# A planner gives the VectorE/GpSimd lock to more operations, and re-ranks by its own plan: a hybrid decoder trunk on one core

## The chip, the core and the metric

The kernel runs on one core of a Trainium2 chip. A core has TensorE (PE: matrix products), VectorE (DVE), ScalarE (ACT), GpSimd (POOL) and SyncE (SP, which issues the transfers here); each works through its own queue of instructions in order, and they meet only at semaphores. SBUF is the on-chip memory that all of them read, PSUM holds the results of TensorE. The metric is the time of one execution on the device in microseconds (us), the median of several runs.

## The reference

Two layers of a decoder trunk on a 1024 x 1024 float32 input. In each layer one input projection feeds four token mixers, whose outputs are normalised, joined, projected and added; then comes a SwiGLU feed-forward block.

```python
for l in range(DEPTH):                      # 2 layers
    h = rmsnorm(x, attn_norm[l])
    proj = h @ w_in[l]                      # 1024 -> 1952 columns, split among the mixers
    y_a = mla_attention(...)                # causal, 4 heads, rotary key
    y_b = short_gated_conv(...)             # width 3
    y_c = multiscale_pool(...)              # trailing means over 2, 4, 8, 16
    y_d = swa_sink_attention(...)           # window 128, sinks, softmax per 128-row block
    mixed = group_rmsnorm(y_a, y_b, y_c, y_d) * mix_norm[l]
    x = x + mixed @ w_o[l]
    h2 = rmsnorm(x, ffn_norm[l])
    gate, up = jnp.split(h2 @ w_gate_up[l], 2, axis=-1)      # 1024 -> 2 x 2816
    x = x + (silu(gate) * up) @ w_down[l]
return rmsnorm(x, final_norm)
```

## The kernel before

Activations are kept transposed, channels on the 128 partitions and 512 tokens in a tile. A product in float32 is made of three fast ones: every operand is split into a rounded high part (a cast on ScalarE, line 301) and the remainder (a subtraction on VectorE, line 304), and TensorE adds high x high, high x low and low x high (the matmuls of line 281). The feed-forward block uses a Strassen-like scheme (the names B11, N1, T3 and so on), whose sums and differences of weights and activations are made on VectorE and, in part, on GpSimd.

The places that matter below, in each of the two layers:

- **Sliding-window attention** (`swa_unit`, 16 units a layer). TensorE makes the scores of a unit (line 594), VectorE adds the bias and finds the row's maximum (line 604), ScalarE takes the exponential (line 617), VectorE adds the sink's part (lines 627, 629, on tiles of 128 x 2), takes the reciprocal (630) and scales the two 128 x 256 halves of the probabilities `tp` by it (line 632, TENSOR_SCALAR); then TensorE transposes them (line 643) and multiplies them with the values (line 655). The matmuls of line 281 that stand between these belong to later projections and fill TensorE's time meanwhile.
- **Sums of two gate/up weight blocks** (`premake`, lines 768 to 776), made early for the feed-forward block: two loads, four GpSimd additions of 128 x 512 (lines 770 to 773), two stores. It is done twice a layer, so eight GpSimd operations stand one behind another.
- **Entry to the feed-forward block.** VectorE makes sums of the normalised activations (lines 1153, 1166, 1172, 1174), splits them and the first weights (line 304, the weights as 128 x 1024), and combines residual tiles (lines 380, 1283); a few additions run on GpSimd (line 1479).

The order of each engine's queue is not written by hand. `scheduled_kernel` records the program once, and `Order` builds a graph of its instructions with two durations for each: `seen` (until its result can be used) and `taken` (until its engine is free). `_forward` is a list scheduler: at each step the engine that is free first takes, of its ready instructions, the one with the smallest rank. It also carries a few shared things, among them `lock`: an operation whose kind is TWO (VectorE) or POOL (a GpSimd TENSOR_TENSOR) begins only when the one before it has released the lock. `find` repeats this with ranks from a backward pass. From its plan PSUM banks and the 47 SBUF slots are given to the tiles (`banks`, `spans`), which adds dependencies of its own, and the program is recorded again; this is done for five rounds, and the round with the shortest plan is kept. Then `_search` perturbs the ranks 1500 times and keeps what `_trials` finds better, the mean of four plans with drawn transfer delays. The order that is left is imposed on the queues.

A GpSimd TENSOR_TENSOR had the kind POOL. On VectorE only a two-tensor operation (TENSOR_TENSOR or SCALAR_TENSOR_TENSOR), both of its inputs with more than two elements a partition, had the kind TWO, when none of these lies in PSUM.

## Time and profile before

| | before |
|---|---|
| median of 3 runs | 2063.58 us (2062.7 to 2064.33) |
| the profiled execution: its time, its span | 2065.29 us, 2063.5 us |
| busy share: TensorE, VectorE, ScalarE, GpSimd | 99%, 76%, 48%, 28% |
| transfers: mean rate over the span | 147 GB/s |

The span runs from the first to the last instruction of the profiled execution; the execution's own time has 1.8 us around it. Each row of a timeline has the start in us, the time in us, engine, line, operation, output and inputs, shape, the count of merged instructions, and, in brackets, how long the engine had stood idle before it and who ended that. Matmuls are pipelined, so that their ends are modelled: the distance from one start to the next says what one costs. Names of tiles stand without their numbers (`u` is a slot of SBUF, `ps_` a PSUM tile). A row of the windows view has, for each engine, the busy time in that stretch and the count of instructions.

### The profile page before, as it was taken

Reading aid. Unit: us, or ns where it says so; the run is one execution under the profiler, and the core shown is the slowest. Engines: PE = TensorE matmul, PEld = TensorE weight load, DVE = VectorE, ACT = ScalarE, POOL = GpSimd, SP = SyncE. Lnnn points to the kernel's source line nnn. Section 1 sums busy time; section 2 is a strip of 40 time slices with the busy share of each in tenths; the row PEclk is TensorE's granted clock in tenths of the full one; section 3 lists DMA queues with packets and bytes.
Section 4 is the critical chain, followed back from the end, with each engine's and each line's share of the span. In section 5 each row is a group of like instructions: output and inputs, shape, how many; then the busy total and the mean of one; then the engine's idle time right before and its main releaser. Section 6 shows DMA issues by size and latency. Waiting matters only on the chain.

```text
span 2063.5 us, 26530 instructions
## 1 busy us (share of the span) xinstructions
PE 2036.2 (99%) x9422; PEld 1679.0 (81%) x9422; DVE 1564.7 (76%) x2443; ACT 992.0 (48%) x1737; POOL 568.5 (28%) x420
## 2 busy tenths in 40 slices
PE   9999999999999999999999999999999999999998
PEld 7787888778888888888887878888788888888887
DVE  8879978998777678655657899789876767785546
ACT  7447647753333334444434476577433333354332
POOL 0100000037687683000001000000578768710000
PEclk9999999999999999999999999999999999999999
DMA  5301222434555556766403002243355555486542
GB/s 207 128 21 36 76 81 83 160 105 169 183 181 172 182 184 240 260 218 222 160 31 125 31 25 89 67 128 118 109 191 175 184 182 178 165 310 239 186 161 100
DMA packets 142117, 302.36 MB, mean 147 GB/s; under 512 B 13856, under 2 KB 60960, under 8 KB 141984
## 3 DMA queue, kind: packets, MB, share of 16 engines
q1 hardware_dynamic: 141984, 300.66, 43.1%
q8 instruction: 74, 1.21, 0.2%
q14 instruction: 59, 0.48, 0.1%
HBM read 212.00 MB, written 87.56 MB: 145 GB/s over the span
## 4 chain that ended last, share of the span: by engine, by line
PE 87%; DVE 6%; ACT 3%; issue 2%; DMA 1%; POOL 0%; SPq 0%; DVEq 0%; ACTq 0%; POOLq 0%
PE ps_mm L281 34%; PE ps_s L281 26%; PE ps_t L281 10%; PE ps_pv L281 8%; PE ps_pv L1065 2%; PE ps_t L1053 1%; DVE u L304 1%; PE ps_s L999 1%; DVE u L307 1%; PE ps_s L1001 1%; PE ps_s L1000 1%; DMA u<-in_w_gu 1%; PE ps_s L871 1%; PE ps_pv L655 1%; ACT u L306 1%
## 5 line engine op out<-in xcount | busy, mean ns | idle before, releaser
L281 PE MATMUL ps_mm<-u,u 128*128 128x512 f32 (+1 forms) x3378 | 839.3, 391 | 4.2 <-DVE u L304 1.7
L281 PEld LDWEIGHTS ps_mm<-u,u 128*128 128x128 f32 x3378 | 618.5, 189 | 130.9 <-issue 5.4
L281 PE MATMUL ps_s<-u,u 128*128 128x512 f32 x2670 | 639.7, 390 | 3.1 <-ACT u L301 1.0
L304 DVE TENSOR_TENSOR u<-u,u 128x1024 fp32r<-128x1024 f32 (+2 forms) x400 | 477.3, 1210 | 167.7 <-ACT u L301 101.8
L281 PEld LDWEIGHTS ps_s<-u,u 128*128 128x128 f32 x2670 | 500.4, 188 | 112.1 <-ACT u L301 2.6
L301 ACT CAST u<-u 128x1024 fp32r<-128x1024 f32 (+2 forms) x400 | 346.8, 882 | 479.0 <-PE ps_s L281 121.5
L281 PE MATMUL ps_t<-u,u 128*128 128x512 f32 (+1 forms) x1124 | 255.8, 377 | 0.5 <-ACT u L306 0.5
L281 PEld LDWEIGHTS ps_t<-u,u 128*128 128x128 f32 x1124 | 202.7, 188 | 40.3 <-ACT u L306 1.3
L1479 POOL TENSOR_TENSOR tp<-tp,u 128x512 f32<-128x512 f32 x80 | 132.3, 1654 | 338.5 <-ACT tp L1477 338.5
L281 PE MATMUL ps_pv<-u,u 128*128 128x512 f32 x744 | 179.2, 389 | 0.1
L281 PEld LDWEIGHTS ps_pv<-u,u 128*128 128x128 f32 x744 | 139.5, 188 | 29.8 <-ACT tn L1342 0.6
L1062 POOL MEMSET u<- 128x128 f32 x32 | 5.7, 206 | 497.9 <-PE ps_mm L281 324.9
L770 POOL TENSOR_TENSOR u<-u,u 128x512 f32<-128x512 f32 x4 | 5.3, 1316 | 373.1 <-PE ps_s L594 288.1
L1477 ACT ACTIVATE tp<-tp 128x512 f32<-128x512 f32 x80 | 50.5, 632 | 109.1 <-DVE tp L380 108.9
L301 ACT CAST u<-ps_t 128x512 fp32r<-128x512 f32 (+3 forms) x132 | 64.4, 502 | 64.3 <-PE ps_t L643 30.1
L304 DVE TENSOR_TENSOR u<-ps_t,u 128x512 fp32r<-128x512 f32 (+3 forms) x132 | 74.5, 580 | 13.6 <-ACT u L301 12.7
L1264 POOL TENSOR_TENSOR u<-u 128x512 f32<-128x512 f32 x38 | 77.8, 2048 | 20.8 <-DVE u L304 20.8
L306 ACT ACTIVATE u<-u,par 128x512 fp32r<-128x512 f32 x100 | 69.8, 715 | 25.5 <-DVE u L380 11.8
L1557 POOL TENSOR_TENSOR u<-u 128x352 f32<-128x352 f32 x64 | 80.6, 1260 | 2.4 <-DMA u<-in_w_dn 1.3
L307 DVE SCALAR_TENSOR_TENSOR u<-u,par,u 128x512 fp32r<-128x512 f32 x100 | 72.9, 746 | 5.0 <-ACT u L306 4.8
L1557 POOL TENSOR_TENSOR u<-u,u 128x352 f32<-128x352 f32 x64 | 74.6, 1165 | 3.6
L345 ACT ACTIVATE tn<-u 128x512 f32<-128x512 f32 (+1 forms) x91 | 52.3, 595 | 43.3 <-DVE u L1750 41.0
(206 smaller groups left out, 2377.2 us busy)
## 6 DMA issues: line engine op xcount, KB each, us to landing
u<-in_w_gu SPq DMA_DIRECT2D x92, 512.0 KB, 3.6
ad<-u SPq DMA_DIRECT2D x154, 256.0 KB, 2.1
u<-ad SPq DMA_DIRECT2D x70, 512.0 KB, 5.8
u<-in_w_dn SPq DMA_DIRECT2D x64, 352.0 KB, 3.2
qd<-u SPq DMA_DIRECT2D x64, 352.0 KB, 3.0
u<-qd SPq DMA_DIRECT2D x32, 512.0 KB, 5.2
u<-in_w_in SPq DMA_DIRECT2D x28, 512.0 KB, 3.8
u<-in_w_dn SPq DMA_DIRECT2D x24, 512.0 KB, 6.5
```

The lines of the kernel that those rows point to most:

```text
L281: pe.matmul(o, w, r, start=start and k == 0 and i == 0, stop=stop and k == n - 1 and i == 2, skip_group_check=again,)
L301: a = act.copy(hi, f)
L304: dve.tensor_tensor(out=lo, in0=f, in1=rd(hi), op=ALU.subtract)
L306: a = act.activation(hi, f, AF.Copy, scale=gain)
L307: dve.scalar_tensor_tensor(out=lo, in0=f, scalar=gain, in1=rd(hi), op0=ALU.mult, op1=ALU.subtract)
L345: act.activation(q, f, AF.Square)
L655: pe.matmul(py[:, (i % 2) * 256 : (i % 2 + 1) * 256], v, R.ap(tt)[:, kb * 256 : (kb + 1) * 256], start=n == 0, stop=n == 2 * nkb - 1,)
L1065: pe.matmul(py[:, c0:], v_of(j, h), R.ap(s)[:, c0:], start=j == 0 and n == 0, stop=j == nj - 1 and n == 1,)
L1264: pool.tensor_tensor(out=q4, in0=q4, in1=F.ap(self.raw[1] + 1), op=ALU.add)
L1477: last_silu = act.activation(g, g, AF.Silu)
L1479: pool.tensor_tensor(out=g, in0=g, in1=r, op=ALU.mult)
L1557: pool.tensor_tensor(out=o, in0=a, in1=b, op=ALU.add)
```

## The change

Four things, all in the planner; the instructions of the program are the same in kind and number.

- The kind TWO is given to every VectorE TENSOR_TENSOR, SCALAR_TENSOR_TENSOR, TENSOR_SCALAR and copy whose inputs all lie in SBUF, whatever their number and size. New in it are the one-input operations (line 632 among them) and those on 128 x 2 tiles (lines 627, 629). The time for which such an operation holds the lock is at least 0.05.
- A transpose on TensorE is put down with 0.1135 instead of 0.109.
- Each of the five rounds is now judged by a short search (a tenth of the trials) and not by `find` alone, and the last search starts from the ranks of the round that won.
- A trial is given up as soon as its sum can't come below the best.

```diff
@@ _forward
-            lock = get + seen[k] - (0.16 if kind[k] == TWO else 0.19)
+            lock = get + max(0.05, seen[k] - (0.16 if kind[k] == TWO else 0.19))
@@ _trials
-def _trials(arrays, graph, lates, order):
+def _trials(arrays, graph, lates, order, limit):
...
         total += end.max()
+        if total + (lates.shape[0] - 1 - s) * (limit - 2.0) > lates.shape[0] * limit:
+            return 1e18
@@ _search
-    best = _trials(arrays, graph, lates, order)
+    best = _trials(arrays, graph, lates, order, 1e9)
...
-        got = _trials(arrays, graph, lates, trial)
+        got = _trials(arrays, graph, lates, trial, best)
@@ Order
+    @staticmethod
+    def tensors(i):
+        return [a for a in i.ins if hasattr(a, "memref")]
...
-        two = op == "TensorTensor" or op == "TensorScalarPtr" and i.is_scalar_tensor_tensor
-        if e == "DVE" and two and len(aps) == 2:
-            return 0 if any(a.memref.startswith("ps_") for a in aps) else TWO
+        if e == "DVE" and op in ("TensorTensor", "TensorScalarPtr", "TensorScalar", "TensorCopy"):
+            return 0 if any(str(a.memref).startswith("ps_") for a in cls.tensors(i)) else TWO
...
             if i.is_transpose:
-                return 0.28, 0.109
+                return 0.28, 0.1135
...
-    def search(self, trials, seed=1):
-        rank = self.find()[1]
+    def search(self, trials, seed=1, rank=None):
+        if rank is None:
+            rank = self.find()[1]
@@ scheduled_kernel
-    for _ in range(rounds):
+    for r in range(rounds):
         _, _, begin, end = plan.find()
         given = plan.banks(begin, end), plan.spans(made, begin, end)
         nc, traced, made = trace(*given)
         plan = Order(traced, nc.dependency_edges)
-        found = plan.find()[0]
-        if best is None or found < best[0]:
-            best = found, given, plan
-    order = best[2].search(trials)[1]
-    return trace(*best[1], order)[0]
+        found = plan.search(trials // 10, r)
+        if best is None or found[0] < best[0]:
+            best = found[0], given, plan, found[4], found[1]
+    _, given, plan, rank, rows = best
+    found = plan.search(trials, rounds, rank)
+    return trace(*given, found[1])[0]
```

What it does to the queues is seen in the order of the built programs. The queues are alike at the start (TensorE's first 100 rows or so) and differ from then on; three places are shown.

**TensorE, layer 0, the last two units of sliding-window attention.** `ps_t<-cst,tp` is a transpose of line 643, which needs the `tp` that line 632 has scaled; `ps_mm` with `u_874`, `u_875` is the projection that stands between; three matmuls belong to each of its pieces of weight (`u_206`, `u_218` and so on, starting at `u_156` behind the last scores). Before:

```order
L281 MATMUL ps_mm<-u_218,u_874 128x512 x2
L281 MATMUL ps_mm<-u_218,u_875 128x512
L643 MATMUL ps_t<-cst,tp 128x128
L281 MATMUL ps_mm<-u_230,u_874 128x512
L643 MATMUL ps_t<-cst,tp 128x128 x3
L281 MATMUL ps_mm<-u_230,u_874 128x512
L281 MATMUL ps_mm<-u_230,u_875 128x512
L643 MATMUL ps_t<-cst,tp 128x128
L281 MATMUL ps_mm<-u_242,u_874 128x512
L643 MATMUL ps_t<-cst,tp 128x128 x2
L655 MATMUL ps_pv<-u_908,u_457 128x256
L643 MATMUL ps_t<-cst,tp 128x128
```

Now:

```order
L281 MATMUL ps_mm<-u_304,u_874 128x512 x2
L643 MATMUL ps_t<-cst,tp 128x128
L281 MATMUL ps_mm<-u_304,u_875 128x512
L281 MATMUL ps_mm<-u_316,u_874 128x512 x2
L281 MATMUL ps_mm<-u_316,u_875 128x512
L281 MATMUL ps_mm<-u_328,u_874 128x512
L643 MATMUL ps_t<-cst,tp 128x128 x3
L281 MATMUL ps_mm<-u_328,u_874 128x512
L281 MATMUL ps_mm<-u_328,u_875 128x512
L281 MATMUL ps_mm<-u_340,u_874 128x512 x2
L281 MATMUL ps_mm<-u_340,u_875 128x512
L655 MATMUL ps_pv<-u_908,u_457 128x256
```

From the last scores to the first transpose stand 25 matmuls of 512 columns instead of 17; then 5 instead of 1 to the other three transposes of that unit; the transposes of the last unit, which followed after 2, now follow after 11 (and 4 matmuls of line 655). The first of the GpSimd additions waits for a matmul that stands 21 places ahead of the end of the last scores (5 of 512 columns and 16 of 256), where it waited for one of these scores themselves.

**TensorE, layer 1, the same place** (`u_9594`, `u_9595` is the projection between). Before:

```order
L281 MATMUL ps_mm<-u_8559,u_9594 128x512 x2
L281 MATMUL ps_mm<-u_8559,u_9595 128x512
L643 MATMUL ps_t<-cst,tp 128x128 x4
L281 MATMUL ps_mm<-u_8867,u_9594 128x512 x2
L281 MATMUL ps_mm<-u_8867,u_9595 128x512
L643 MATMUL ps_t<-cst,tp 128x128 x4
L281 MATMUL ps_mm<-u_8628,u_9594 128x512 x2
```

Now:

```order
L655 MATMUL ps_pv<-u_9530,u_9178 128x256 x4
L281 MATMUL ps_mm<-u_8810,u_9594 128x512
L643 MATMUL ps_t<-cst,tp 128x128
L281 MATMUL ps_mm<-u_8810,u_9594 128x512
L281 MATMUL ps_mm<-u_8810,u_9595 128x512
L281 MATMUL ps_mm<-u_8559,u_9594 128x512 x2
L281 MATMUL ps_mm<-u_8313,u_9724 128x512 x2
L643 MATMUL ps_t<-cst,tp 128x128 x3
L281 MATMUL ps_mm<-u_8559,u_9595 128x512
L281 MATMUL ps_mm<-u_8867,u_9594 128x512 x2
L281 MATMUL ps_mm<-u_8867,u_9595 128x512
L281 MATMUL ps_mm<-u_8628,u_9594 128x512 x2
```

The last unit's transposes followed 3 matmuls behind those of the unit before; now 13 matmuls of 512 columns and 4 of 256 stand between. The two rows with `u_8313,u_9724` begin another product, in a PSUM bank that VectorE's line 480 must have read; in VectorE's queue that operation stands right behind the pair of line 632. Of the GpSimd additions the first waits for a matmul that stands 18 places ahead of the end of the first scores (6 of 512 columns, 8 of 256, 4 transposes).

**VectorE, layer 0, entry to the feed-forward block.** `u_4404` (128 x 1024) is the remainder of the first weights. Before:

```order
L380 TENSOR_TENSOR tp<-ps_t,u_3957 128x512
L1166 SCALAR_TENSOR_TENSOR tp<-u_3186,par,te 128x512
L304 TENSOR_TENSOR u_4340<-tp,u_4340 128x512
L1283 TENSOR_TENSOR u_3957<-ps_t,tn 128x512
L1153 SCALAR_TENSOR_TENSOR tp<-tp,te 128x512
L304 TENSOR_TENSOR u_4404<-u_4401,u_4403 128x1024
```

Now:

```order
L380 TENSOR_TENSOR tp<-ps_t,u_3957 128x512
L1166 SCALAR_TENSOR_TENSOR tp<-u_3186,par,te 128x512
L304 TENSOR_TENSOR u_4340<-tp,u_4340 128x512
L304 TENSOR_TENSOR u_4404<-u_4401,u_4403 128x1024
L1153 SCALAR_TENSOR_TENSOR tp<-tp,te 128x512
L304 TENSOR_TENSOR u_4360<-tp,u_4360 128x512
```

The remainder of the weights has come two places forward, ahead of lines 1283 and 1153. In layer 1 the same operations keep their places, but line 1283 has come ahead of all of them.

## The prediction

> **What bounds the kernel now.** I read the page's first part and its chain first, then the busy time by stretches of the span, then who TensorE waits for, then the timelines of the places where it waits.

> ```profile
> span 2063.5 us, 26530 instructions
> PE 2036.2 (99%) x9422; PEld 1679.0 (81%) x9422; DVE 1564.7 (76%) x2443; ACT 992.0 (48%) x1737; POOL 568.5 (28%) x420
> PE 87%; DVE 6%; ACT 3%; issue 2%; DMA 1%; POOL 0%; SPq 0%; DVEq 0%; ACTq 0%; POOLq 0%
> ```

> TensorE is busy for 2036.2 of 2063.5 us and carries 87% of the chain. The instructions do not change, so the busy time stays; all that another order can win lies in the 27.3 us in which TensorE is idle. Where they are, by stretches (PE first, then weight load, VectorE, ScalarE, GpSimd):

> ```profile
> 0.00:50.00 50.00, 47.84 (x212) 38.25 (x213) 43.97 (x72) 39.40 (x66) 0.20 (x4) 1.00 0.59 213
> 50.00:100.00 50.00, 45.68 (x231) 37.78 (x231) 41.81 (x106) 20.53 (x61) 10.20 (x8) 0.93 0.37 132
> 400.00:500.00 100.00, 97.86 (x421) 79.26 (x420) 90.80 (x108) 48.90 (x75) 43.87 (x29) 0.98 0.35 117
> 500.00:600.00 100.00, 100.00 (x443) 82.84 (x442) 72.34 (x70) 35.04 (x48) 73.82 (x52) 1.00 0.57 185
> 1100.00:1200.00 100.00, 96.69 (x473) 78.92 (x473) 80.81 (x190) 49.89 (x122) 10.18 (x8) 0.98 0.17 61
> 1400.00:1500.00 100.00, 96.94 (x419) 77.43 (x418) 93.17 (x125) 58.67 (x93) 32.54 (x19) 1.00 0.34 118
> 2000.00:2063.50 63.50, 54.10 (x362) 49.63 (x360) 37.15 (x69) 18.99 (x37) 0.00 (x0) 0.94 0.24 82
> ```

> The feed-forward stretch (500 to 600) has no gap: 443 matmuls in 100 us, 0.226 us for one of 512 columns. GpSimd and its lock cost nothing there, however VectorE is slowed. The head (2.16 us idle) and the tail (9.40) are the fill and drain; the queues are alike in the first, and the last chain is the same. That leaves 15.7 us, of which 4.32 lie at 50 to 100, 3.31 at 1100 to 1200, 2.14 and 3.06 at the two entries to the feed-forward block. Who TensorE waits for (total, times, longest):

> ```profile
> PE ps_t L643 <- DVE tp L632: 7.4, 7, 1.7
> PE ps_mm L281 <- DVE u L304: 1.7, 1, 1.7
> ```

> The largest by far is the transposes' wait for line 632. Its place in layer 0: GpSimd's first and last addition, VectorE, and TensorE with its idle time in brackets.

> ```profile
> 85.39 1.30 POOL L770 TENSOR_TENSOR u<-u,u 128x512 f32<-128x512 f32 x1 [84.95 <-DVE u L672]
> 94.64 1.27 POOL L773 TENSOR_TENSOR u<-u 128x512 f32<-128x512 f32 x1
> 84.23 0.69 DVE L380 TENSOR_TENSOR u<-u,te 128x512 f32<-128x512 f32 x1
> 87.08 0.88 DVE L627 TENSOR_TENSOR sm<-sm,par 128x2 f32<-128x2 f32 x1
> 89.57 2.52 DVE L632 TENSOR_SCALAR tp<-tp,sm 128x256 f32<-128x256 f32 x2
> 92.01 1.23 DVE L629 TENSOR_TENSOR sm<-sm,sm 128x2 f32<-128x2 f32 x1
> 93.48 2.58 DVE L632 TENSOR_SCALAR tp<-tp,sm 128x256 f32<-128x256 f32 x2
> 84.37 1.12 PE L594 MATMUL ps_s<-u,u 128*128 128x256 f32 x8
> 85.33 4.04 PE L281 MATMUL ps_mm<-u,u 128*128 128x512 f32 x17
> 90.95 0.30 PE L643 MATMUL ps_t<-cst,tp 128*128 128x128 f32 x1 [1.58 <-DVE tp L632]
> 92.14 0.55 PE L643 MATMUL ps_t<-cst,tp 128*128 128x128 f32 x3 [0.66 <-DVE tp L632]
> 92.45 0.71 PE L281 MATMUL ps_mm<-u,u 128*128 128x512 f32 x2
> 94.86 0.45 PE L643 MATMUL ps_t<-cst,tp 128*128 128x128 f32 x1 [1.70 <-DVE tp L632]
> 96.11 0.69 PE L643 MATMUL ps_t<-cst,tp 128*128 128x128 f32 x2 [0.38 <-DVE tp L632]
> L632 DVE TENSOR_SCALAR tp<-tp,sm x64: 277/347/1429, 53.6 to 1192.1; 128x256 f32<-128x256 f32 x56, 128x128 f32<-128x128 f32 x8
> ```

> A scaling of line 632 takes 347 ns (the median in the last row), but 2.52 for two while GpSimd adds: each waits for the GpSimd operation that is running. So does a 128 x 2 operation of line 629, at 1.23. These are the operations to which the planner gave no lock: it put 17 matmuls (17 x 0.226 = 3.85 us) where 5.6 were needed. In layer 1 the same (GpSimd's first addition, TensorE's three waits, and a VectorE operation used below):

> ```profile
> 1109.96 1.30 POOL L770 TENSOR_TENSOR u<-u,u 128x512 f32<-128x512 f32 x1 [288.12 <-PE ps_s L594]
> 1115.43 0.55 PE L643 MATMUL ps_t<-cst,tp 128*128 128x128 f32 x3 [0.81 <-DVE tp L632]
> 1118.04 0.30 PE L643 MATMUL ps_t<-cst,tp 128*128 128x128 f32 x1 [1.36 <-DVE tp L632]
> 1119.28 0.55 PE L643 MATMUL ps_t<-cst,tp 128*128 128x128 f32 x3 [0.95 <-DVE tp L632]
> 1115.30 0.68 DVE L480 SCALAR_TENSOR_TENSOR te<-ps_mm,u 128x512 f32<-128x512 f32 x1
> ```

> **The change part by part.** No instruction is added or taken away. The floor of 0.05, the transposes' 0.1135, the early end of trials and the seeds cost nothing on the chip, since they act through the order alone.

> *Layer 0, the softmax beside GpSimd.* Waits removed at most: 1.58 + 0.66 + 1.70 + 0.38 = 4.32 us. What stays? I take the end of the scores, 85.33, as the mark. A matmul of 256 columns costs 0.12 ((85.33 - 84.37) / 8), a transpose 0.10 ((92.45 - 92.14) / 3). GpSimd now starts 5 x 0.226 + 16 x 0.12 = 3.05 us earlier against the mark, less the 0.69 for which line 380, ready in that time, takes the lock: 2.4 earlier, so that its last addition ends at 95.91 - 2.4 = 93.5. The two scalings of the first unit ended with GpSimd's fourth and fifth addition (four from 85.39, about 1.32 apart: 90.7; then 92.09). The softmax can't be ready earlier than before (line 627 at 87.08), so it loses two places in GpSimd's row of eight: scalings end with the sixth and seventh addition at 90.9 and 92.2, plus 0.35 each. TensorE comes to the first transpose at 85.33 + 25 x 0.226 = 90.98 and to the other three 0.10 + 5 x 0.226 = 1.23 later, so it waits 0.3 and 0.1. If VectorE misses one place more, 1.3 is added: 1.7 at most. The last unit's transposes come 11 x 0.226 + 4 x 0.12 = 3.0 us later, after GpSimd is done, and wait for nothing. I take 1.0, between the ends: **-3.3** (-4.3 to -2.6; if the shift of GpSimd fails because the second pair of weight blocks lands late, -2).

> *Layer 1.* Waits removed at most: 0.81 + 1.36 + 0.95 = 3.12. GpSimd starts 6 x 0.226 + 8 x 0.12 + 4 x 0.10 = 2.7 us ahead of the first scores' end. The last unit's transposes gain 13 x 0.226 + 4 x 0.12 = 3.4 us, which covers 1.36 + 0.95 whole. The first unit's have 17 + 3 matmuls and 12 of 256 columns (20 x 0.226 = 4.5 + 0.9) against 20 and 4 before, so their wait goes from 0.81 to about nothing. But two matmuls ahead of the last three transposes need a bank that line 480 reads, and that stands behind the two scalings: where these end late, its 0.68 and about 0.4 of a slot at GpSimd come to TensorE, up to 1.1. I take 0.8: **-2.3** (-3.1 to -1).

> *Entry to the feed-forward block.* VectorE is the bound there:

> ```profile
> 400.00:420.00 20.00, 20.00 (x89) 16.19 (x88) 20.00 (x30) 13.91 (x23) 1.30 (x1) 1.00 0.14 46
> 432.49 0.68 DVE L1283 TENSOR_TENSOR u<-ps_t,tn 128x512 f32<-128x512 f32 x1
> 433.09 1.16 DVE L1153 SCALAR_TENSOR_TENSOR tp<-tp,te 128x512 f32<-128x512 f32 x1
> 434.17 1.21 DVE L304 TENSOR_TENSOR u<-u,u 128x1024 fp32r<-128x1024 f32 x1
> 1452.14 3.96 POOL L1479 TENSOR_TENSOR tp<-tp,u 128x512 f32<-128x512 f32 x1 [11.76 <-ACT tp L1477]
> 1456.13 0.69 DVE L380 TENSOR_TENSOR u<-ps_t,tp 128x512 f32<-128x512 f32 x1 [1.19 <-POOL tp L1479]
> ```

> It is busy for 20.00 of 20 us, so TensorE gets its operand as VectorE's queue comes to it. In layer 0 the remainder of the weights comes forward past lines 1283 and 1153, which took 434.17 - 432.49 = 1.68 us. What may take some of it back is the next thing late, line 380 behind a GpSimd addition of line 1479: it stood 1.19 for that in layer 1. So -1.7 to -0.5, and I take **-1.0**. In layer 1 line 1283 has come ahead of the same remainder, which is 433.09 - 432.49 = 0.60 later: **+0.6**.

> [...]

> *All the rest.* 15.7 - 7.4 - 2.1 - 3.1 = 3.1 us of idle time lie scattered; another order makes others of the same kind. I take 0, with 2.5 either way.

> Sum: -3.3 - 2.3 - 1.0 + 0.6 = -6.0. The profiled execution was 2065.29 us (span 2063.5 and 1.8 around it), 1.7 above the median of the runs, 2063.58. So 2059.3 for such an execution, and **2057.6** for the median.

> **The rivals.**

> *The search finds more.* It re-ranks 750 times more and picks the slot plan by a searched time; if it also halves the rest (the 5.2 at the two entries and 3.1 elsewhere), 4 more go: 2053.5. For it: a lock known is a lock that can be planned around. Against: layer 1's entry stands almost as it stood. 15%.

> *The stalls move.* The same 10.2 us of GpSimd work holds off the same VectorE operations; if the second weight pair lands late, or line 480 and the scores behind it take over the wait, about 2 us are won: 2061.6. Against: 25, 5 and 13 matmuls are real cover. 20%.

> *The change does not do what it says*: the lock for one-input operations is a fiction, or binds nowhere. The rows at 89.57 and 92.01 show it binding, and the queues did move there, so this has 2%; the time would be that of a random re-order, 2063.

> *Slower: GpSimd starves behind VectorE's trains.* The planner hands the lock to GpSimd after one VectorE operation; the row at 1452.14 shows 3.96 - 1.30 = 2.66 us lost behind a train of them, with line 380 waiting after it and TensorE behind that. If the new order sends all four additions of line 1479 at the two entries (two in each layer) into such trains, 4 x 2.66 = 10.6 us come back, against the 6.0: 2068.2. It decides from the third on (3 x 2.66 = 8 against 6). Against it: line 1479 has moved by a place or two only. 6%.

> **How the numbers follow.** Likeliest, my sum: 57%, with 2055 to 2060.5 by its terms' ends. Less than 0.2% (4.1 us) can't be told from no change here, so faster means under 2059.5 and slower over 2067.7. Faster: most of the 57% (47) and the 15% of the search: 0.62. Slower: 0.05. The rest, 0.33, is the upper part of the sum's range and the stalls that move. The range reaches to both neighbours, 2052.5 to 2063.

> **What would show it.** In the new profile the wait of line 643 for line 632 should fall from 7.4 to under 3 us; TensorE's busy time at 50 to 100 should rise by about 3 us, and at 1100 to 1200 by 2; GpSimd's first addition should start some 2.5 us ahead of the last scores. At the entries, idle time of about 1 us in layer 0 and 3.7 in layer 1. I am wrong if the wait of line 643 stays over 5, if a new row of TensorE's waits stands over 2 us, or if the 500 to 1000 stretch is no longer full.

## The result, and the profile after

| | before | after |
|---|---|---|
| median (lowest to highest) | 2063.32 us (2062.7 to 2064.33, 4 runs) | 2049.36 us (2049.12 to 2049.48, 4 runs) |
| profiled execution: time, span | 2065.29, 2063.5 us | 2049.12, 2047.3 us |

The ratio is 0.9932 (95% interval 0.9915 to 0.9949). Beside the experiments below both were timed again: 2048.80 against 2066.26 us, ratio 0.9915 (0.9902 to 0.9929). The two medians of before lie 3 us apart, within the 7.6 us over which its runs spread (last section). The direction was as predicted, the size was not: 14.0 us by the medians where 6.0 were forecast, and a time below the range. The span fell by 16.2 us.

The first part of the page of after:

```profile
span 2047.3 us, 26523 instructions
PE 2030.1 (99%) x9422; PEld 1675.2 (82%) x9422; DVE 1552.7 (76%) x2443; ACT 992.3 (48%) x1737; POOL 574.1 (28%) x420
```

TensorE's idle time fell from 27.3 to 17.2 us, that is by 10.1, and its busy time from 2036.2 to 2030.1, by 6.1, with the same 9422 matmuls. The second number is the surprise. After, by the same stretches as in the prediction (span, TensorE's busy time first; the third column from the right is the granted clock):

```profile
50.00:100.00 50.00, 50.00 (x265) 42.22 (x264) 41.08 (x109) 22.64 (x64) 10.62 (x8) 1.00 0.39 132
400.00:500.00 100.00, 98.46 (x429) 79.74 (x428) 84.78 (x100) 48.08 (x72) 56.55 (x36) 1.00 0.42 138
500.00:600.00 100.00, 100.00 (x443) 82.81 (x442) 71.96 (x71) 34.86 (x47) 72.06 (x51) 1.00 0.53 174
1100.00:1200.00 100.00, 99.56 (x479) 80.16 (x478) 85.13 (x191) 56.39 (x127) 5.13 (x5) 1.00 0.14 49
1400.00:1500.00 100.00, 97.14 (x425) 78.75 (x424) 89.39 (x113) 52.58 (x81) 45.15 (x28) 1.00 0.35 120
2000.00:2047.30 47.30, 37.99 (x289) 36.17 (x287) 24.29 (x51) 10.33 (x22) 0.00 (x0) 0.95 0.25 90
```

At 50 to 100 no idle time is left, at 1100 to 1200 0.44 us, and the clock, which read 0.93, 0.98 and 0.98 in three of these rows before, is 1.00 everywhere but in the tail. Who TensorE waits for now, longest first:

```profile
PE ps_mm L281 <- DVE u L304: 1.9, 2, 1.7
PE ps_s L281 <- DVE u L304: 1.6, 2, 0.9
PE ps_pv L497 <- DVE ones L155: 1.1, 1, 1.1
```

The row of line 643 waiting for line 632 (7.4 us before) is gone; what leads now is the wait at the entry to the feed-forward block and the drain. The place in layer 0, in the timeline of after:

```profile
83.49 1.30 POOL L770 TENSOR_TENSOR u<-u,u 128x512 f32<-128x512 f32 x1 [83.05 <-PE ps_mm L281]
93.12 1.30 POOL L773 TENSOR_TENSOR u<-u 128x512 f32<-128x512 f32 x1
89.64 0.74 DVE L629 TENSOR_TENSOR sm<-sm,sm 128x2 f32<-128x2 f32 x1
91.55 1.64 DVE L632 TENSOR_SCALAR tp<-tp,sm 128x256 f32<-128x256 f32 x2
85.86 0.64 PE L594 MATMUL ps_s<-u,u 128*128 128x256 f32 x4
86.34 5.86 PE L281 MATMUL ps_mm<-u,u 128*128 128x512 f32 x25
92.04 0.30 PE L643 MATMUL ps_t<-cst,tp 128*128 128x128 f32 x1
93.33 0.49 PE L643 MATMUL ps_t<-cst,tp 128*128 128x128 f32 x3
```

The scalings still stand behind GpSimd (1.64 us for two), but 25 matmuls run meanwhile, and the transposes come when their operands are there: no brackets, no idle time.

### The profile page after: what moved, and what is told of

Its sections match the earlier page's. It is cut to its first block, busy times and chain, and to the rows that moved or that the text cites. A ratio compares the mean times of both kernels' runs of the same rounds, so it can differ in the third digit from the quotient of the medians.

```text
span 2047.3 us, 26523 instructions
## 1 busy us (share of the span) xinstructions
PE 2030.1 (99%) x9422; PEld 1675.2 (82%) x9422; DVE 1552.7 (76%) x2443; ACT 992.3 (48%) x1737; POOL 574.1 (28%) x420
## 3 DMA queue, kind: packets, MB, share of 16 engines
q8 instruction: 74, 1.21, 0.2%
## 4 chain that ended last, share of the span: by engine, by line
PE 86%; DVE 7%; ACT 2%; issue 2%; DMA 1%; POOL 0%; SPq 0%; DVEq 0%; ACTq 0%; POOLq 0%
PE ps_mm L281 33%; PE ps_s L281 27%; PE ps_t L281 10%; PE ps_pv L281 8%; PE ps_pv L1065 2%; PE ps_t L1053 1%; DVE u L307 1%; DVE u L304 1%; PE ps_s L999 1%; DVE u L353 1%; PE ps_s L1000 1%; PE ps_s L1001 1%; PE ps_s L871 1%; PE ps_pv L655 1%; PE ps_s L594 1%
## 5 line engine op out<-in xcount | busy, mean ns | idle before, releaser
L281 PE MATMUL ps_mm<-u,u 128*128 128x512 f32 (+1 forms) x3378 | 835.4, 390 | 2.6 <-DVE u L304 1.9
L281 PEld LDWEIGHTS ps_mm<-u,u 128*128 128x128 f32 x3378 | 614.9, 188 | 129.8 <-issue 4.6
L281 PE MATMUL ps_s<-u,u 128*128 128x512 f32 x2670 | 636.8, 390 | 2.4 <-DVE u L304 1.6
L304 DVE TENSOR_TENSOR u<-u,u 128x1024 fp32r<-128x1024 f32 (+2 forms) x400 | 470.5, 1192 | 175.5 <-ACT u L301 107.7
L281 PEld LDWEIGHTS ps_s<-u,u 128*128 128x128 f32 x2670 | 500.4, 188 | 110.0 <-DVE u L304 2.4
L281 PE MATMUL ps_t<-u,u 128*128 128x512 f32 (+1 forms) x1124 | 255.9, 377 | 0.1
L281 PEld LDWEIGHTS ps_t<-u,u 128*128 128x128 f32 x1124 | 202.5, 188 | 40.5 <-DVE u L307 0.9
L1479 POOL TENSOR_TENSOR tp<-tp,u 128x512 f32<-128x512 f32 x80 | 139.5, 1744 | 337.4 <-ACT tp L1477 337.4
L281 PE MATMUL ps_pv<-u,u 128*128 128x512 f32 x744 | 178.3, 389 | 0.1
L281 PEld LDWEIGHTS ps_pv<-u,u 128*128 128x128 f32 x744 | 139.3, 188 | 29.9 <-ACT tn L1342 1.0
L770 POOL TENSOR_TENSOR u<-u,u 128x512 f32<-128x512 f32 x4 | 5.2, 1292 | 365.9 <-PE ps_mm L281 365.9
L1477 ACT ACTIVATE tp<-tp 128x512 f32<-128x512 f32 x80 | 50.5, 632 | 97.1 <-DVE tp L380 97.0
L304 DVE TENSOR_TENSOR u<-ps_t,u 128x512 fp32r<-128x512 f32 (+3 forms) x132 | 75.0, 581 | 15.1 <-ACT u L301 13.9
L380 DVE TENSOR_TENSOR tp<-tp,u 128x512 f32<-128x512 f32 x76 | 71.8, 945 | 2.0
```

The lines of the kernel that those rows point to most:

```text
L281: pe.matmul(o, w, r, start=start and k == 0 and i == 0, stop=stop and k == n - 1 and i == 2, skip_group_check=again,)
L304: dve.tensor_tensor(out=lo, in0=f, in1=rd(hi), op=ALU.subtract)
L380: dve.tensor_tensor(out=o, in0=a, in1=b, op=ALU.mult)
L1477: last_silu = act.activation(g, g, AF.Silu)
L1479: pool.tensor_tensor(out=g, in0=g, in1=r, op=ALU.mult)
```

## Where 6 us of busy time went

TensorE's clock had been halved three times inside the kernel before. The profile keeps the granted clock as intervals: before it was 0.5 at 93.14 to 99.97, 434.47 to 437.89 and 1120.55 to 1123.97 us, after at no time between 5 us and the drain. All of these are one or two times 3.413 us long, and they start on one grid of 3.413 us. Before, cut on that grid (clock in the third column from the right, TensorE's busy time first behind the length):

```profile
89.73:93.14 3.41, 1.52 (x7) 0.83 (x7) 3.41 (x3) 0.78 (x4) 3.41 (x3) 1.00 0.47 193
93.14:96.56 3.42, 1.34 (x6) 0.85 (x5) 3.35 (x5) 0.23 (x1) 2.61 (x3) 0.50 0.62 216
96.56:99.97 3.41, 3.41 (x13) 2.97 (x12) 1.79 (x4) 1.62 (x3) 0.00 (x0) 0.50 0.61 245
99.97:103.38 3.41, 3.41 (x18) 2.85 (x17) 1.80 (x4) 1.07 (x4) 0.00 (x0) 1.00 0.00 0
431.06:434.47 3.41, 1.78 (x6) 0.59 (x4) 3.41 (x6) 1.87 (x4) 1.39 (x1) 1.00 0.00 0
434.47:437.89 3.42, 2.94 (x7) 2.37 (x8) 3.42 (x6) 0.42 (x1) 0.00 (x0) 0.50 0.43 137
1117.14:1120.55 3.41, 1.57 (x8) 1.28 (x9) 2.75 (x4) 0.59 (x1) 3.15 (x3) 1.00 0.48 181
1120.55:1123.97 3.42, 3.42 (x11) 2.84 (x11) 2.00 (x3) 1.23 (x2) 0.00 (x0) 0.50 0.83 302
```

Each of the three windows at full clock ahead of a half-clock one here had TensorE idle for 1.63 to 1.89 us by its busy time (over 2.1 by the distances between starts, last section). At half clock matmuls of 512 columns begin 0.427 us apart, where they begin 0.227 apart at full clock, and count as busy: 11 matmuls fill the 3.42 us of the last row. The busy time of the four half-clock windows is 1.34 + 3.41 + 2.94 + 3.42 = 11.1 us; half of that, 5.6 by the granted clock of 0.50, is the clock's, and TensorE's busy time fell by 6.1. (The difference is small beside the modelled ends: the profiles of all the kernels below that keep at most one half-clock window and have no matmuls or holds added show busy times from 2028.6 to 2030.5.) So a stall was paid twice: once as idle time, and again in the 3.4 us behind it. That this is so, and that the lock is behind it, had to be tested.

## The experiments

The theories: **A**, the planner's knowledge of the lock puts matmuls ahead of the waiting transposes, and this takes away both the idle time and the half clock behind it. **B**, the half clock costs nothing of its own; **C**, it has nothing to do with the idle time; **D**, the gain is the search's; **E**, any other order moves by some us; **F**, line 632 is late for other reasons than GpSimd. The kernel before, timed beside these runs, had medians of 2066.26 to 2066.67 us; the ratios are against those.

### TensorE kept busy in the stall, in the plan of before

```diff
+FILL = {  # layer, group, unit: (matmuls, unit and transpose they stand ahead of)
+    (0, 0, 6): ((6, 6, 0),),
+    (0, 0, 7): ((2, 6, 1), (7, 7, 0)),
+    (1, 0, 7): ((3, 6, 1), (5, 7, 0)),
+}
...
+                    m = pe.matmul(pt, ones_r, R.ap(vs[g][1]), start=True, stop=True)
```

> The plan of before, unchanged, with 23 matmuls of 512 columns (5.2 us of TensorE's time, results overwritten) put ahead of the transposes that wait for line 632. VectorE, GpSimd and all waits for line 632 stay, so no work is ready earlier; only TensorE isn't idle there. Theory A (the idle time itself was only part of the loss, and the clock that is halved behind it the rest): the granted clock is 1.00 at 84 to 105 and 1105 to 1124, TensorE's busy time without the fillers falls by some 3.5 us, and the time is 2058 to 2061. Rival B (the clock's dip costs nothing of its own, since TensorE would have waited there anyway): 2063 to 2065. Rival C (the dips have nothing to do with the idle time): the clock dips at the same places.

Measured: 2060.52 us (2059.6 to 2060.89), ratio 0.9968 (0.9956 to 0.9981). The kernel does 23 matmuls more and is faster. The first part of its page:

```profile
span 2059.0 us, 26573 instructions
PE 2038.2 (99%) x9445; PEld 1682.9 (82%) x9445; DVE 1568.1 (76%) x2443; ACT 991.9 (48%) x1737; POOL 568.7 (28%) x420
```

The two softmax stretches (columns as above):

```profile
50.00:100.00 50.00, 48.82 (x255) 40.44 (x255) 42.51 (x106) 20.73 (x62) 10.27 (x8) 1.00 0.36 132
1100.00:1200.00 100.00, 98.51 (x484) 80.34 (x483) 82.33 (x190) 51.35 (x123) 10.21 (x8) 1.00 0.17 61
```

The transposes' wait for the scalings (lines 654 and 639 here):

```profile
PE ps_t L654 <- DVE tp L639: 2.1, 3, 1.0
```

The clock is 1.00 in both stretches; the half-clock interval at the entry (433.90 to 437.31), where no matmul was put, stays. Without the fillers' 5.2 us TensorE is busy for 2033.0, 3.2 less than before. B and C fall: idle time was the cause of the half clock, and the half clock cost time.

### GpSimd's additions made short, in the plan of before

```diff
+            c = slice(0, 8 if narrow else HT)
+            kept = w1 if narrow else q
...
-            pool.tensor_tensor(out=F.ap(q + 1), in0=a21, in1=a22, op=ALU.add)
+            pool.tensor_tensor(out=q1[:, c], in0=a21[:, c], in1=a22[:, c], op=ALU.add)
```

> Before, in its own plan and order, but the 16 GpSimd additions of premake are made on 8 columns instead of 512 (in place, stored from there), so that the weight sums are left out of the computation; nothing else moves. Theory A (line 632 is late because GpSimd holds the lock): a scaling takes 0.35 us everywhere, the wait of line 643 falls from 7.4 to under 1.5, the clock stays at 1.00 in the two windows, and the time falls by 7.4 of idle time and 3.5 of half clock, to about 0.995 of before. Rival F (the scalings are late for what VectorE does before them, not for GpSimd): the wait stays over 4 us and the time within 0.1% of before.

Measured: 2053.93 us (2051.57 to 2054.64), ratio 0.9937 (0.9924 to 0.9949). Lines 632 and 629 by shape (shortest, median and longest duration in ns):

```profile
L632 DVE TENSOR_SCALAR tp<-tp,sm x64: 268/347/355, 54.6 to 1180.4; 128x256 f32<-128x256 f32 x56, 128x128 f32<-128x128 f32 x8
L629 DVE TENSOR_TENSOR sm<-sm,sm x32: 148/156/161, 54.2 to 1177.7; 128x2 f32<-128x2 f32 x32
```

The two stretches:

```profile
50.00:100.00 50.00, 50.00 (x264) 42.06 (x264) 39.54 (x111) 22.90 (x65) 2.72 (x8) 1.00 0.39 132
1100.00:1200.00 100.00, 99.78 (x488) 81.37 (x488) 83.73 (x197) 56.55 (x130) 0.90 (x4) 1.00 0.20 64
```

The longest scaling falls from 1429 to 355 ns, the 128 x 2 operation's longest from 1232 (the row of before has 145/157/1232) to 161, and the wait of line 643 leaves the list. F falls: in these two stretches the long scalings were GpSimd's doing. The gain was larger than expected, since the half clock at the entry of layer 0 is gone too. That is luck: the idle time at 400 to 500 is as before (2.16 against 2.14 us), and the windows cut it otherwise, with 1.90 us at most in one against 2.36 before. Some idle time came back elsewhere (0.93 us more at 1400 to 1500).

### One part of the change at a time

The new kinds alone (with the floor of 0.05), and again with another seed of the last search:

```diff
-        two = op == "TensorTensor" or op == "TensorScalarPtr" and i.is_scalar_tensor_tensor
-        if e == "DVE" and two and len(aps) == 2:
-            return 0 if any(a.memref.startswith("ps_") for a in aps) else TWO
+        if e == "DVE" and op in ("TensorTensor", "TensorScalarPtr", "TensorScalar", "TensorCopy"):
+            return 0 if any(str(a.memref).startswith("ps_") for a in cls.tensors(i)) else TWO
```

> Before with only the new kinds (and the floor of 0.05): the slot plan is chosen and the ranks are searched as before. Theory A (knowing the lock of the one-input and 128 x 2 operations puts work ahead of the waiting transposes, and that is the gain): the wait of line 643 for line 632 falls under 3 us, no half clock in the two windows, 2050 to 2056. Rival D (the gain is the search's, the best of five slot plans and the re-ranking): the wait stays over 4 us, 2060 to 2065. Rival E (a draw of luck, any changed plan moves by some us): neither, 2054 to 2066 with waits elsewhere.

> The new kinds alone with another seed of the last search. If the 4 us between the kinds alone and the changed kernel are luck of one draw, this one may fall anywhere from 2047 to 2056; if the short search of five slot plans (or the transposes' cost) makes them, it stays at 2051 to 2054.

The search alone (after without the kinds, the floor and 0.1135):

> After without the new kinds, the floor and the 0.1135: only the best of five searched slot plans, the re-ranking and the early end of trials. Theory A: the wait of line 643 for line 632 stays at 5 to 8 us with the half clock behind it, 2060 to 2064. Rival D: 2050 to 2055. Rival E: 2054 to 2066, the wait at line 632 by chance.

Before with another seed (`search(trials, 2)`):

> Before with another seed of its last search, so another order of the same quality by the old planner. Theory A: the planner doesn't know the lock of line 632, so the wait there is again 5 to 9 us and the time 2061 to 2066. Rival E: the time moves by over 4 us, and the wait at line 632 falls under 4 by luck.

The wait of line 643 for line 632 is read from the list of TensorE's waits, the half clock from the intervals of the granted clock:

| kernel | median, us | ratio to before (95%) | line 643 waits for 632, us | half clock inside, windows |
|---|---|---|---|---|
| new kinds alone | 2052.91 | 0.9933 (0.9919 to 0.9946) | 1.6 | 1 (entry, layer 1) |
| the same, another seed | 2052.11 | 0.9933 (0.9919 to 0.9947) | 1.8 | 0 |
| search alone | 2066.52 | 1.0001 (0.9992 to 1.0010) | 7.8 | 4 |
| before, another seed | 2066.79 | 1.0003 (0.9995 to 1.0012) | 7.6 | 6 |

The two stretches under the search alone:

```profile
50.00:100.00 50.00, 45.67 (x236) 37.80 (x235) 40.53 (x106) 21.02 (x63) 10.19 (x8) 0.97 0.34 121
1100.00:1200.00 100.00, 96.53 (x468) 78.68 (x467) 82.19 (x190) 49.46 (x119) 10.19 (x8) 0.97 0.17 61
```

and under the kinds alone:

```profile
50.00:100.00 50.00, 49.09 (x259) 41.27 (x258) 40.74 (x108) 21.86 (x63) 10.25 (x8) 1.00 0.37 128
1100.00:1200.00 100.00, 98.86 (x475) 80.02 (x474) 86.17 (x194) 56.01 (x128) 9.02 (x8) 1.00 0.16 58
```

D and E fall as explanations of the main gain. Three orders by the old planner (before, search, another seed) lie within 0.03% of each other, with 7.4 to 7.8 us of that wait and 4 to 6 half-clock windows; both orders by the new kinds lie 14 us lower. A search can't plan around a delay that its model doesn't have.

### What the rest of the change adds, and which kind matters

The changed kernel beside these runs, and with another seed; and with the transposes at 0.109 again:

> The changed kernel again, beside the others and on their chip. If the new kinds are all of it (theory A), its ratio to before is that of the run with the kinds alone, 0.993, or 2 to 3 us better by what the longer search adds once the kinds are known: 2049 to 2053. If the search gives nothing there either, the two agree within 1 us.

> The changed kernel with another seed of its last search. Theory A: the wait of line 643 for line 632 stays under 2 us, no half clock at 50 to 100 and 1100 to 1200, 2047 to 2054. Rival E (luck): another order of the same planner lies 4 us or more away from it, up to 2060.

> The changed kernel with the transposes put down at 0.109 again: the new kinds and the longer search. If the 4 us by which the changed kernel beats the kinds alone come from the search, the time is that of the changed kernel, 2048 to 2050. If from the transposes' 0.1135 (or from the draw of another plan), 2051 to 2054.

Only the one-input TENSOR_SCALAR of the new kinds, in the old search:

```diff
+        if e == "DVE" and not two and op in ("TensorScalarPtr", "TensorScalar") and cls.size(i.outs[0]) > 2:
+            return 0 if any(str(a.memref).startswith("ps_") for a in cls.tensors(i)) else TWO
```

> Before with only one of the new kinds: the one-input TENSOR_SCALAR from SBUF (line 632 above all) takes the lock, the 128 x 2 operations and copies don't, and the search is the old one. If line 632 is what matters: the time of all kinds alone, 2051 to 2054 (ratio 0.993), the wait of line 643 for line 632 under 2.5 us. If the 128 x 2 operations matter as much (each takes a slot at GpSimd, 1.23 us for line 629 in the trace of before): a wait of 3 to 5 us is left, with a half-clock window in one of the two places, 2056 to 2061.

| kernel | median (lowest to highest), us | ratio to before (95%) |
|---|---|---|
| changed kernel again | 2048.80 (2048.75 to 2049.57) | 0.9915 (0.9902 to 0.9929) |
| the same, another seed | 2048.48 (2047.15 to 2049.22) | 0.9913 (0.9900 to 0.9927) |
| transposes at 0.109 | 2051.03 (2050.49 to 2051.59) | 0.9927 (0.9915 to 0.9940) |
| only TENSOR_SCALAR | 2056.43 (2053.78 to 2058.68) | 0.9952 (0.9938 to 0.9966) |

By the medians the kinds alone give 13.8 of the 17.5 us and the whole change 3.7 more. The draw of the last search doesn't make these 3.7: the two seeds with the kinds alone lie at 2052.91 and 2052.11, those of the whole change at 2048.80 and 2048.48. How they divide between the longer search, the 0.1135 and the slot plan that was picked is not settled. With the kinds and the longer search but 0.109 the time is 2051.03, just inside the branch that gives the 3.7 to the 0.1135 or to another plan. Its profile is like that of the kinds alone: 0.92 and 1.07 us idle in the two softmax stretches (0.91 and 1.14 there, 0.00 and 0.44 in after), 1.8 us of the wait of line 643, and a half-clock window at the entry of layer 1 (1437.76), which the profiles of the changed kernel and of its other seed don't have. So the kinds and the longer search together did not bring all of the 3.7 here; but this is one slot plan. Line 632's kind alone gives 10 of the 13.8. Neither branch of that expectation held whole: the wait left is 2.2 us and the profiled execution has no half clock, as if line 632 were all, but the median is that of the other branch. The profiled execution is the fastest of the five (2053.78); the slower ones, at a mean clock down to 0.997, were not looked into. The 4 us that are missing would be those of the 128 x 2 operations and the copies; but it is one plan, and the intervals of the two ratios overlap. Of its idle time 2.23 and 1.50 us lie in the two softmax stretches, 1.7 more than with all the kinds; where the rest comes from stays open.

### Holds of known length where TensorE is never idle

The changed kernel, with 24 places in the feed-forward blocks at which the next matmul waits for a chain of small copies on ScalarE:

```diff
+        held.extend([act.copy(hold, hold).ins for _ in range(n)] for _, n in HOLDS)
...
+                    Order.tie(tc, group[0], pe[x], mybir.DependencyClass.Sync)
+                    Order.tie(tc, pe[x + 1], group[-1], mybir.DependencyClass.Sync)
```

> The changed kernel with 24 holds in the feed-forward blocks, where TensorE is otherwise never idle: at each the next matmul waits for a chain of 1 to 12 small copies on ScalarE (some 0.6 to 3 us). Theory G (the clock is set once per 3.41 us, and halves for the next 3.41 us where TensorE was idle for more than about 2 us of the last): holds under 1.8 us are never followed by half clock, holds near 3 us mostly are, and each such costs 1.7 us more than the hold. Rival H (a whole window must be idle, more than 3.4 us): no hold is followed by half clock, and the time is that of the holds alone.

Measured: one execution of 2101.92 us, span 2100.1. The waits for the holds (total, times, longest; line 169 makes the copies):

```profile
PE ps_mm L292 <- ACT hold L169: 15.7, 8, 2.8
PE ps_s L292 <- ACT hold L169: 11.9, 9, 2.8
PE ps_pv L292 <- ACT hold L169: 8.5, 4, 2.8
PE ps_t L292 <- ACT hold L169: 2.6, 3, 1.2
```

The granted clock was halved for one window each behind five of the 24 holds. Two holds with the windows around them, on the grid of this execution:

```profile
871.80:875.22 3.42, 1.63 (x8) 1.01 (x6) 1.25 (x3) 1.79 (x9) 0.00 (x0) 1.00 0.62 205
875.22:878.63 3.41, 3.31 (x14) 2.73 (x15) 0.92 (x1) 0.04 (x1) 0.00 (x0) 1.00 0.01 5
...
909.35:912.76 3.41, 1.06 (x5) 0.67 (x4) 0.24 (x1) 1.98 (x10) 0.00 (x0) 1.00 0.70 274
912.76:916.17 3.41, 3.41 (x9) 2.64 (x8) 2.14 (x3) 1.47 (x2) 0.00 (x0) 0.50 0.00 0
916.17:919.59 3.42, 3.42 (x16) 2.82 (x15) 1.23 (x1) 0.23 (x1) 0.00 (x0) 1.00 0.73 207
```

The first hold leaves TensorE idle for 1.95 us of its window (by the distances from one matmul's start to the next, less the 0.226 of one), and the window behind it does 14 matmuls. The second, 2.62 us, is followed by a window at 0.50 with 9 matmuls instead of 16. All five holds that were followed by half clock had over 2.3 us in one window. Two of nearly 3 us, which an edge of the grid split (1.77 and 1.20; 2.02 and 0.94), were not: so in these holds it was the idle time within a window that counted, not the gap. H falls.

The price agrees as well. The span is 52.3 us longer than the changed kernel's in the same set of runs (2047.8). The four rows of waits add up to 38.7, and TensorE's busy time grew by 13.1 (2030.2 to 2043.3): 5 x 1.7 = 8.5 of it is the half clock, and the remaining 4.6, 0.19 for each hold, is about the rest of the last matmul ahead of it, whose end is otherwise covered by the next (an estimate: a matmul of line 281 is put down with 0.39 us on the pages, and the next starts 0.226 after it: 0.16).

## Why the prediction was wrong, point by point

**The step that failed** is the second sentence on the bound: "the instructions do not change, so the busy time stays; all that another order can win lies in the 27.3 us in which TensorE is idle". The instructions stayed, 9422 matmuls, and the busy time did not: it fell by 6.1 us (2036.2 to 2030.1), and the fillers, which changed nothing but whether TensorE was idle there, took 3.2 of it away. The rows that say so were quoted in the prediction itself: 0.93 at 50 to 100, 0.98 at 400 to 500, 0.98 at 1100 to 1200, read over as a column that doesn't matter. (1 - 0.93) x 50 + 0.02 x 100 + 0.02 x 100 = 7.5 us of lost clock (6.8 by the intervals) was the bound of the missing term. The page's row of clock digits shows nothing of it: 0.93 prints as a 9. With the idle term as measured but the busy time kept, the forecast would have been 2063.6 - 10.1 = 2053.5, still 4 us too high (2065.3 - 10.1 = 2055.2 against 2049.1 for the two profiled executions, where the 6.1 are missing whole). The idle time, forecast to fall by 6.0, fell by 10.1; term by term:

**Layer 0's softmax**, -3.3 forecast: idle time at 50 to 100 went from 4.32 to 0.00, the end of the range. The mechanism was as told: GpSimd starts 2.85 us ahead of the end of the scores (83.49 against 86.34; some 2.5 promised), and 25 matmuls cover the scalings. The 1.0 that was kept for a place missed in GpSimd's row didn't come. **Layer 1**, -2.3: 3.31 to 0.44, -2.9; line 480 took nothing that shows.

**The entries**, -1.0 and +0.6: 2.14 to 1.54 and 3.06 to 2.86, so -0.6 and -0.2. The sign of the second was wrong: the 0.60 that line 1283 was to cost does not show. The first fell short for the reason that the forecast allowed for: in layer 0, too, an addition of line 1479 now stands behind VectorE's operations (2.73 us, where the one before line 380 took 1.39 before), line 380 waits 1.19 for it, and TensorE waits behind that. In layer 1 it is as it was. From after's timelines, layer 0 first:

```profile
423.53 2.73 POOL L1479 TENSOR_TENSOR tp<-tp,u 128x512 f32<-128x512 f32 x1 [13.59 <-ACT tp L1477]
426.29 0.69 DVE L380 TENSOR_TENSOR u<-ps_s,tp 128x512 f32<-128x512 f32 x1 [1.19 <-POOL tp L1479]
427.64 1.21 PE L281 MATMUL ps_s<-u,u 128*128 128x512 f32 x4 [0.66 <-DVE u L304]
1435.51 3.96 POOL L1479 TENSOR_TENSOR tp<-tp,u 128x512 f32<-128x512 f32 x1 [11.77 <-ACT tp L1477]
1439.50 0.69 DVE L380 TENSOR_TENSOR u<-ps_t,tp 128x512 f32<-128x512 f32 x1 [1.19 <-POOL tp L1479]
```

**The rest**, 0 with 2.5 either way: -10.1 + 4.32 + 2.87 + 0.60 + 0.20 = -2.1, inside its bounds.

**The rivals.** "The search finds more" named nearly the right time of the idle part, but for another reason: the search alone is worth nothing (1.0001), and only with the kinds in place does the rest of the change add its 3.7 us, by a way that is not settled. "The stalls move": no new row of waits stands over 2 us. "The change does not do what it says" is excluded by the run with the kinds alone. "GpSimd starves": two such additions instead of one, the one at the entry of layer 1 as before and that of 2.73 us in layer 0; the price of the new one is the 0.66 us above.

**The signs.** The wait of line 643 fell below 3 (to nothing), and 500 to 1000 stayed full. TensorE's busy time, promised to rise by 3 and 2 at the two softmax stretches, rose by 4.3 and 2.9. But these rises show the idle time alone: at 50 to 100 the count of matmuls rose from 231 to 265, by 29 of 512 columns, 3 of 256 and 2 of 128. At 0.226, 0.12 and 0.10 us that is 7.1 us of work, where 4.32 us were idle. Most of the difference is the clock, (1.34 + 3.41) / 2 = 2.4 us by the windows, which a busy share does not show.

## What to carry to other kernels

## What the runs showed of the hardware

**Half clock followed windows with 2.10 us or more of idle time of TensorE, in one gap or in pieces.** In 13 profiled executions (one of each kernel here, two of the changed one), windows on the 3.413 us grid that ran at full clock, between 10 us and the drain:

| idle time of TensorE in the window | windows | followed by half clock |
|---|---|---|
| 1.83 to 2.02 us (54 to 59%) | 12 | 0 |
| 2.10 to 3.01 us (62 to 88%) | 18 | 18 |

The idle time is taken as in the holds, from distances between starts of matmuls. The longest single gap in one of the 18 was as short as 0.90 us (before, 431.06 to 434.47: 2.36 us idle in pieces), while a gap of 2.96 us that lay over two windows halved nothing. A window that is itself at half clock is another matter: that of 93.14, busy for 1.34 of 3.42 us, was followed by a second, that of 434.47, busy for 2.94, was not. Where that bound lies stays open.

**The times of before, with stalls near that bound, spread most.** The grid isn't tied to the start of the kernel (in the 13 profiles a window begins 0.26 to 3.40 us behind the first instruction, 0.98 in before and 1.72 in after), so the same stall may fall into one window or be split over two, as two of the holds were (1.77 and 1.20; 2.02 and 0.94). The 21 runs of before in one set spread over 7.6 us (2062.4 to 2069.98), the 5 of the changed kernel over 0.8 and the 5 of the fillers' over 1.3. Of the 21, the five at a mean clock of 0.994 have a median of 2067.10 and the six at 0.996 one of 2063.89, but they overlap; that the number of half-clock windows makes the spread is argued from this, not shown run by run.

**The lock binds small and one-input operations.** A 128 x 2 VectorE operation of 0.16 us took up to 1.23 us beside GpSimd's additions and never over 0.161 with these made short. Line 632 has one tensor input, and its 355 ns against 1429 show that it waits too. These are times inside an operation, not idle time ahead of it: so, other than the section on the chip has it, VectorE and GpSimd did not meet only at semaphores here. In the trace of before a one-input scaling (line 1037: 345, 412 and 483 ns for 256, 384 and 512 columns) costs 0.54 ns a column, and a subtraction with two inputs (line 304, one of them in PSUM: 418, 551 and 685 ns) 1.04. Whether that difference has to do with why line 632 waits is not shown: no run tests it.
